# A decoder block on one core: the compression's row loads become steps of their own, and the gated unit's temporaries move to another buffer

## The chip, the cores and the metric

The kernel runs on one core of a Trainium2 chip. The metric is the device time of one execution in microseconds (us). Engines are named as in the profile: PE (matrix products; PEld is its weight load), DVE (vector), ACT (scalar functions; it also issues weight loads), POOL, and SP, which issues most of the other transfers.

## The reference

One decoder block over 512 tokens of width 1024: a half-step SwiGLU layer of inner width 2816, a mixing stage, a second SwiGLU layer, a gate with a per-layer embedding and a final norm. The mixing stage joins sparse attention (8 heads of 64, three branches) and a state-space mixer (S5) that ends in a gated unit. What the change touches, cut from the reference:

```python
def compress(kv, pe, w1, w2):            # done for keys and for values
    tok = arange(n_cmp)[:, None] * 16 + arange(32)[None, :]
    blk = kv[:, tok] + pe                # 31 windows of 32 tokens, stride 16
    ...
    return gelu(blk @ w1) @ w2
...
kc = compress(k_cmp, ...); vc = compress(v_cmp, ...)
...
def s5_mixer(...):
    ...
    y = gelu(y)
    return y * sigmoid(y @ w_glu + b_glu)
...
h = h + concat(o_nsa, o_s5) @ w_out
```

## The kernel before

All of it is one program on one core, tokens along the free axis, in tiles of 128 rows by 512 tokens. The two SwiGLU layers and the large projections split every weight tile into two parts, `hi` and `lo` (an ACT cast at L164 and a DVE subtraction at L166), and do three products for each pair of tiles. Weight tiles come through a ring of four buffers named `raw` (L107, issued by ACT).

The change lies in the mixing stage, at 400 to 620 us of the span. The stage is written as Python generators, each a chain of steps: `s` the state-space mixer, `q`, `Q` and `k` the projections with rotary embedding of queries and keys, `z` (`cmp_kv`) the projections of the keys and values that are to be compressed, `v` (`v_gates`) the values and branch gates, `p` and `t` the loading of queries and the scores of a block of 128 of them, `c` (`cmp_all`) the compression, `g` (`glu`) the gated unit, `f` the half of the output projection that reads the gated unit, `V` the products with the values. The string `PLAN` sets the order in which the steps are written down; a scheduler then places the instructions of each engine, earlier-written work first among what it holds to be ready. So a moved step shifts its neighbours on every engine too.

Steps pass results through small buffers with tags. Two tiles of one tag share memory, and the later one waits for all readers of the earlier. In the pool `tp` there is one buffer for each of `r1`, `r2`, `rb1`, `r3`; the rotary steps, the gated unit and the compression all use them.

- `cmp_kv` writes rotated keys to `kcd` (L1082) and values to `vcd` (L1087) in device memory.
- `windows` (L1114) reads them back in shifted copies: for each of two groups a tile `cst` in tag `r1` or `r2`, in two loads (L1118, L1119). Then DVE adds the position table `pe` (L1125) into `cs` (keys, tags `rb1` and `r3`) or into `turn` (values).
- `cmp_all` calls `windows` for keys and values in its first step; eight steps of matrix products `ps_A<-raw,cs` and `ps_A<-raw,turn` follow, and a last step with a gelu in `rb1`, a hidden tile `chid` in tag `acc` of the pool `npool` (L1153), and small products into `KAc` and `VLc`.
- `glu` runs a gelu over each of four tiles `yt` (function `gelu2`, L918: Square on ACT, a DVE step at L922, Tanh on ACT, a DVE step at L924), with its temporary `gt` in tags `r1`, `r2`, `r1`, `r2`. Then come sixteen products `ps_A<-yt,raw`, four for each of four results, the fourth of them reading the fourth `yt`. `f` needs all four results.

The first three gelus are written before the compression, the fourth well after it.

Of the kernel before, what the change touches and what calls it, by code (L numbers as in the profile page):

```python
# [10 lines left out]
F32 = mybir.dt.float32  # L11
# [8 lines left out]
SEQ = 512  # L20
# [56 lines left out]
def block_kernel(ctx: ExitStack, tc: tile.TileContext, a: dict, out: bass.AP):  # L77
# [14 lines left out]
    def bank(tag, shape=(128, 512), dt=F32):  # L92
        return psum.tile(list(shape), dt, tag=tag, name="ps_" + tag)
# [38 lines left out]
    def mm(o, lhsT, rhs, start, stop, **kw):  # L132
        return PE.matmul(o, lhsT, rhs, start=start, stop=stop, **kw)  # L133
# [10 lines left out]
    def unit(raw_only=False, keep=None, q=nc.scalar, after=None, at=None):  # L144
        i = unit_i[0] if at is None else at
        if at is None:
            unit_i[0] += 1
        w = UNIT_W[i]
        if i not in raws:
            load_unit(i, q)  # L150
        raw = raws.pop(i)
        if raw_only:
            return raw
        return split(raw, (slice(0, w),), keep, after)
# [25 lines left out]
    npool = ctx.enter_context(tc.tile_pool(name="npool", bufs=1, side="right"))  # L180
# [631 lines left out]
    with ExitStack() as f1:  # L812
# [5 lines left out]
        sp = s5c.enter_context(tc.tile_pool(name="s5c", bufs=1, side="right", reuse_waits="tile"))  # L818
# [25 lines left out]
    kcd = dram.tile([64, 2, SEQ], F32, tag="kcd", name="kcd")  # L844
    vcd = dram.tile([2, 64, SEQ], F32, tag="vcd", name="vcd")

    def mixer(ctx):
# [29 lines left out]
        tp = ctx.enter_context(tc.tile_pool(name="tmp", bufs=1, reuse_waits="tile"))  # L877
# [36 lines left out]
        def act(*args, **kw):  # L914
            with tc.issue_after(table[0].ins):
                S.activation(*args, **kw)

        def gelu2(o, x, w, tag):  # L918

            t = tp.tile([128, SEQ], F32, tag=tag, name="gt")[:, :w]  # L920
            act(t, x, AF.Square)
            V.scalar_tensor_tensor(t, t, 1 / 0.044715, x, OP.add, OP.mult)  # L922
            act(t, t, AF.Tanh, scale=math.sqrt(2 / math.pi) * 0.044715)
            V.scalar_tensor_tensor(o, t, 1.0, x, OP.add, OP.mult)  # L924
# [32 lines left out]
        cosr, sinr = turn[:, 0], turn[:, 1]  # L957
# [156 lines left out]
        def windows(src, i, dst):  # L1114
            ev = []
            for g in range(2):
                st = tp.tile([128, SEQ], F32, tag=f"r{g + 1}", name="cst")
                nc.sync.dma_start(st[0:64], src[g])  # L1118
                nc.sync.dma_start(st[64:128, 0:SEQ - 1], src[g, :, 1:SEQ])  # L1119
                ev.append(st.rearrange("p (j l r) -> p l j r", l=8, r=2)[:, :, :, 0])  # L1120
            sp = []
            for half, t in enumerate(dst):
                t = t.rearrange("p (l g j) -> p l g j", l=8, g=2)
                for g in range(2):
                    V.tensor_tensor(t[:, :, g], ev[g],  # L1125
                                    pe[:, i, 8 * half:8 * half + 8, None].to_broadcast([128, 8, 32]), OP.add)
                sp.append(t)
            return sp

        def cmp_all():  # L1130

            kt = [tp.tile([128, SEQ], F32, tag=n, name="cs") for n in ("rb1", "r3")]
            sps = windows(kcd.rearrange("(g r) a t -> g (r a) t", g=2), 0, kt), windows(vcd, 1, (cosr, sinr))
            yield
            ps = bank("A", (128, 256))
            for l in range(16):
                if l % 2 == 0:
                    raw = unit(True, at=next(at["cmp"]))
                lo, n = l // 8, 64 - l // 8
                for i in range(2):  # L1140
                    xs = sps[i][lo][:, l % 8].rearrange("p g j -> p (g j)")[:, lo:64]
                    w = (2 * i + l % 2) * 256
                    mm(ps[64 * i:64 * i + n], xs, raw[:, w:w + 256], l == 0, l == 15)
                if l % 2:
                    yield
            KBc = state["KBc"] = mp.tile([128, 4, 2, 128], FR, tag="turn", name="KBc")
            G.dma_start(KBc.rearrange("p q g j -> p (q g j)"), a["kbc"])
            ht = tp.tile([128, SEQ], F32, tag="r3", name="ht")[:, :256]
            gelu2(ht, ps, 256, "rb1")
            pt = bank("C", (128, 2, 128))  # L1150
            for m in range(2):
                PE.transpose(pt[:, m], ht[:, m * 128:m * 128 + 128], ident)
            hid = npool.tile([128, SEQ], F32, tag="acc", name="chid", bufs=1)[:, :256].rearrange("p (m c) -> p m c", m=2)  # L1153
            S.activation(hid, pt, AF.Copy, scale=0.5)
            hk, hv = hid[:, :, 0:63], hid[:, :, 64:127]
            p = bank("D", (64, 2, 32))
            for m in range(2):
                mm(p.rearrange("p g j -> p (g j)")[:, 0:63], w2[:, 0, m], hk[:, m], m == 0, m == 1)
            p = p[:, :, 0:31]
            kah = KAc[:, 0:128].rearrange("p (g i j) -> p g i j", g=2, i=2)  # L1160
            S.copy(kah[0:64, :, 0, 0:31], p)
            S.copy(kah[64:128, :, 0, 0:31], p)
            V.tensor_tensor(kah[0:64, :, 1, 0:31], p, kah[0:64, :, 0, 0:31].bitcast(F32), OP.subtract)
            for g in range(2):
                V.tensor_copy(KBc[0:64, :, g, 0:31],
                              kah[0:64, g:g + 1, 1, 0:31].bitcast(F32).to_broadcast([64, 4, 31]))
            for g in range(2):
                p = bank("D", (31, 64))
                for m in range(2):
                    mm(p, hv[:, m, 32 * g:32 * g + 31], w2[:, 1, m], m == 0, m == 1)  # L1170
                S.copy(VLc[0:31, g, 0:64], p)
                V.tensor_tensor(VLc[0:31, g, 64:128], p, VLc[0:31, g, 0:64].bitcast(F32), OP.subtract)


        def glu():
            for m in range(4):
                yt = yts[m]
                gelu2(yt, yt, SEQ, GT[m % 2])
                yield
            for m in range(4):  # L1180
                if m % 2 == 0:
                    raw = unit(True, at=next(at["glu"]))
                o = bank("A")
                for k in range(4):
                    q = (m * 4 + k) % 8
                    mm(o, raw[:, q * 128:(q + 1) * 128], yts[k], k == 0, k == 3)
                sg = mp.tile([128, SEQ], F32, tag="ra", name="sg", bufs=2)

                act(sg, o, AF.Tanh, scale=0.25, bias=bglu[:, m:m + 1])
                V.scalar_tensor_tensor(sg, sg, 1.0, yts[m], OP.add, OP.mult)  # L1190
                S.activation(oh[:, 4 + m], sg, AF.Copy, scale=0.25)
                V.scalar_tensor_tensor(ol[:, 4 + m], sg, 0.25, oh[:, 4 + m].bitcast(F32), OP.mult, OP.subtract)
                yield
# [132 lines left out]
        def values(qb, env):  # L1326
# [3 lines left out]
            for g in range(2):  # L1330
# [39 lines left out]
                for par in range(2):  # L1370
# [7 lines left out]
        envs = {qb: {} for qb in range(4)}  # L1378
        gens = dict(u=s5_input(), k=keys(), q=rotary("q0", qd[0], TQ[0]), Q=rotary("q1", qd[1], TQ[1]), z=cmp_kv(),
                    v=v_gates(), s=s5_all(), c=cmp_all(), g=glu(), f=out_half(range(4, 8)))  # L1380
        made = {"p": lambda b: queries(b, mp if b > 1 else ap_), "t": lambda b: scores(b, TS[b]),
                "x": lambda b: compressed(b), "V": lambda b: values(b, envs[b])}
        table.append(tc.keep_in_program_order(S.preload_act_table_set("exp_and_others")))
        for step in PLAN.split():
            if step == "close":
# [43 lines left out]
    for m in range(KT):  # L1429
# [3 lines left out]
        for k in range(2):  # L1433
            q = (m * 2 + k) % 8
# [16 lines left out]
    with tc.tile_pool(name="gate", bufs=2, reuse_waits="tile") as gp:  # L1451
# [8 lines left out]
        acc = npool.tile([128, SEQ], F32, tag="acc", name="accf", bufs=1)  # L1460
# [119 lines left out]
TU, TQ, TW, TY, TP = "AD", "AA", "C", "D", "D"  # L1580

TS = "AB", "AB", "BC", "BBBBBBBBBCBCBCBC"
GT = "r1", "r2"
STAGE = ("ra", "ra"), ("ra", "ra"), ("ra", "ra"), ("ra", "ra")

PLAN = """u u u k s s u k k q s q s Q p3 s s s k s Q s t3 t3 s t3 z t3 s s t3 s p3 s z t3 t3 s s t3 t3 s g t3 g t3 g t3
v t3 c v v c t3 v c c p2 t2 t3 t3 t2 p2 c c c t2 c c t2 t2 c v t2 t2 t2 t2 t2 t2 t2 t2 t2 g close p1 p1 p0 x3  # L1590
p0 g t2 g t2 g g t1 t1 x2 f S2 t1 f t1 t1 f t1 t1 f f t0 t0 R2 f x1 t0 R3 V3 V3 V3 V3 V3 V3 V3 V3 V3 V3 V3 V3
V3 V3 V3 V3 x0 f V3 t1 V3 V3 V2 V2 V2 V2 V2 t0 V2 V2 V2 V2 V2 S0 V2 R1 R0 V2 V2 V2 V2 V1 V1 V1 V1 V1 V1 V1
# [167 lines left out]
```

## Time and profile before

| | us |
|---|---|
| median of 3 runs (lowest, highest) | 1046.03 (1044.05, 1049.57) |
| the profiled execution, its own time | 1045.87 |
| its span | 1044.1 |
| DVE, ACT, POOL busy in the span | 823.1, 502.0, 160.5 |
| window loads `cst`, issue to landing, lowest/median/highest | 2.5/3.9/4.3 |

The profile's busy time of PE counts a matmul until its modelled end, and the records of neighbours overlap. So a waiting PE shows either as idle time ahead of a row, or as fewer matmuls in a stretch than in another with matmuls of the same size. A row of the timeline gives start, duration, engine, line and operation, and in brackets the idle time of that engine before it and what ended it.

### The profile page before, as it was taken

The page shows a single profiled execution, that of the slowest core. Times are in us where ns is not written, and L with a number is a line of the kernel's source. Part 1 is how long each engine was busy: PE and PEld are TensorE (multiplying, and loading weights), DVE is VectorE, ACT ScalarE, POOL GpSimd, SP SyncE. Part 2 cuts the span into 40 slices and gives each one's busy share as a digit, 9 for nine tenths or more (in the row PEclk, how much of TensorE's full clock was granted, in tenths as well). Part 3 has the DMA queues.
Part 4 walks back from the last instruction along what each step waited for, and adds up shares of the span by engine and source line. Part 5 has one row for each costly group of instructions (what it writes and reads, how often), then busy time and mean ns, then how long its engine had stood idle before and what let it go on. Part 6 is the DMA issues. An engine that isn't in the chain of part 4 may idle for free.

```text
span 1044.1 us, 15711 instructions
## 1 busy us (share of the span) xinstructions
PE 1030.6 (99%) x6049; PEld 876.9 (84%) x6049; DVE 823.1 (79%) x1381; ACT 502.0 (48%) x868; POOL 160.5 (15%) x181
## 2 busy tenths in 40 slices
PE   9999999999999999999999999999999999999997
PEld 7888888889889888776586688898899899899886
DVE  6798468988989766896689887996598588587666
ACT  6322232535336542477768855653365246245452
POOL 0003948207870200100000000000000000000001
PEclk9999999999999999999999999999999999999999
DMA  7424325636354648766610023434234333333412
GB/s 265 144 91 128 99 89 171 226 121 129 119 138 146 227 122 226 209 194 171 200 41 21 20 61 121 132 111 121 85 100 121 101 102 101 101 102 101 133 69 81
DMA packets 53114, 131.55 MB, mean 126 GB/s; under 512 B 10800, under 2 KB 19664, under 8 KB 53040
## 3 DMA queue, kind: packets, MB, share of 16 engines
q10 hardware_dynamic: 26352, 90.77, 27.4%
q0 software_dynamic: 6592, 18.48, 7.0%
q1 hardware_dynamic: 20096, 21.31, 6.7%
q8 instruction: 47, 0.77, 0.3%
q14 instruction: 27, 0.22, 0.1%
HBM read 114.39 MB, written 15.73 MB: 125 GB/s over the span
## 4 chain that ended last, share of the span: by engine, by line
PE 85%; DVE 5%; POOL 3%; DMA 3%; ACT 2%; issue 2%; SPq 0%; DVEq 0%; ACTq 0%; POOLq 0%
PE ps_A L133 25%; PE ps_C L133 24%; PE ps_B L133 20%; PE ps_D L133 15%; POOL ft L721 1%; POOL bt L720 1%; DMA qf<-qd 1%; DMA qd<-r 1%; DVE lo L166 1%; DMA kf<-kd 1%; DVE el L1359 0%; DMA cst<-kcd 0%; POOL ft L719 0%; DVE s L342 0%; POOL seen L559 0%
## 5 line engine op out<-in xcount | busy, mean ns | idle before, releaser
L164 ACT CAST hi<-raw 128x1024 fp32r<-128x1024 f32 (+2 forms) x143 | 144.4, 1010 | 253.3 <-PE ps_C L133 92.5
L133 PE MATMUL ps_C<-hq,hi 128*128 128x512 f32 x704 | 217.5, 390 | 0.2
L166 DVE TENSOR_TENSOR lo<-raw,hi 128x1024 fp32r<-128x1024 f32 (+2 forms) x143 | 173.4, 1213 | 42.5 <-ACT hi L164 41.5
L133 PEld LDWEIGHTS ps_C<-hq,hi 128*128 128x128 f32 x704 | 130.8, 188 | 28.1 <-DVE h L526 1.4
L133 PE MATMUL ps_C<-hq,lo 128*128 128x512 f32 x352 | 136.9, 389 | 0.0
L133 PE MATMUL ps_A<-xh,hi 128*128 128x512 f32 (+1 forms) x352 | 124.8, 355 | 0.4 <-ACT hi L164 0.4
L133 PE MATMUL ps_A<-xl,hi 128*128 128x512 f32 (+1 forms) x352 | 123.9, 352 | 0.0
L133 PE MATMUL ps_A<-xh,lo 128*128 128x512 f32 (+1 forms) x352 | 122.9, 352 | 0.2 <-DVE lo L166 0.2
L164 ACT CAST hi<-s 128x1024 fp32r<-128x1024 f32 x56 | 58.9, 1053 | 107.0 <-PE ps_D L133 60.9
L166 DVE TENSOR_TENSOR lo<-s,hi 128x1024 fp32r<-128x1024 f32 x56 | 70.6, 1261 | 20.3 <-ACT hi L164 20.2
L133 PEld LDWEIGHTS ps_C<-hq,lo 128*128 128x128 f32 x352 | 66.1, 188 | 13.8
L133 PEld LDWEIGHTS ps_A<-xh,hi 128*128 128x128 f32 x352 | 66.6, 189 | 10.3 <-ACT hi L164 0.7
L133 PEld LDWEIGHTS ps_A<-xh,lo 128*128 128x128 f32 x352 | 66.6, 189 | 9.2 <-DVE lo L166 0.4
L133 PEld LDWEIGHTS ps_A<-xl,hi 128*128 128x128 f32 x352 | 66.6, 189 | 9.3 <-DVE xl L192 0.3
L526 DVE SCALAR_TENSOR_TENSOR h<-ps_C,h 128x512 f32<-128x512 f32 x64 | 43.9, 686 | 36.5 <-PE ps_C L133 36.3
L133 PE MATMUL ps_B<-sh,lo 128*128 128x256 f32 x224 | 63.1, 282 | 0.3 <-DVE lo L166 0.3
L133 PE MATMUL ps_D<-sl,hi 128*128 128x256 f32 x224 | 63.1, 282 | 0.0
L133 PE MATMUL ps_B<-sh,hi 128*128 128x256 f32 x224 | 63.0, 281 | 0.0
L133 PE MATMUL ps_B<-sl,hi 128*128 128x256 f32 x224 | 62.9, 281 | 0.0
L133 PE MATMUL ps_B<-xh,hi 128*128 128x512 f32 (+1 forms) x168 | 62.9, 374 | 0.0
L133 PE MATMUL ps_D<-sh,hi 128*128 128x256 f32 x224 | 62.8, 280 | 0.0
L133 PE MATMUL ps_D<-sh,lo 128*128 128x256 f32 x224 | 62.6, 280 | 0.0
(434 smaller groups left out, 2472.1 us busy)
## 6 DMA issues: line engine op xcount, KB each, us to landing
raw<-in_wpack ACTq DMA_DIRECT2D x168, 512.0 KB, 3.6
si<-s5i POOLq DMA_DIRECT2D x8, 512.0 KB, 5.3
so<-s5o POOLq DMA_DIRECT2D x8, 512.0 KB, 5.7
h<-in_xT SPq DMA_DIRECT2D x8, 256.0 KB, 4.5
s5i<-fs POOLq DMA_DIRECT2D x1, 2048.0 KB, 11.4
xraw<-in_xT SPq DMA_DIRECT2D x8, 256.0 KB, 3.6
s5o<-gt POOLq DMA_DIRECT2D x1, 2048.0 KB, 13.3
s5i<-tcs POOLq DMA_DIRECT2D x2, 1024.0 KB, 10.2
```

The costliest lines, as they stand in the source:

```text
L133: return PE.matmul(o, lhsT, rhs, start=start, stop=stop, **kw)
L164: p, q = S.copy(hi[:, c], raw[:, c]), None
L166: q = V.tensor_tensor(lo[:, c], raw[:, c], hi[:, c].bitcast(F32), OP.subtract)
L526: V.scalar_tensor_tensor(h[:, m, :], o[m], 0.5, h[:, m, :], OP.mult, OP.add)
L720: G.tensor_tensor(bt, b2[:, 1], bc(psn[:, e]), OP.mult)
L721: G.tensor_tensor(ft[:, :, s_, :], ft[:, :, s_, :], bt, OP.add)
```

## The change

`windows` becomes a generator with two steps: the loads, then the adds. `cmp_all` gets two steps more: loads of the keys' rows; their adds and the loads of the values' rows; the values' adds. `PLAN` gets two more `c`. The first stands right behind the second `z`, the second behind the first gelu of the gated unit; the old first place now holds the values' adds. The temporaries of the gated unit move from `r1` and `r2` to the one buffer `acc` of `npool`, which `chid` also uses. No instruction is added or removed.

```diff
-            t = tp.tile([128, SEQ], F32, tag=tag, name="gt")[:, :w]
+            t = (npool if tag == "acc" else tp).tile([128, SEQ], F32, tag=tag, name="gt", bufs=1)[:, :w]
...
                 ev.append(st.rearrange("p (j l r) -> p l j r", l=8, r=2)[:, :, :, 0])
+            yield
             sp = []
...
-            return sp
+            yield sp
...
-            sps = windows(kcd.rearrange("(g r) a t -> g (r a) t", g=2), 0, kt), windows(vcd, 1, (cosr, sinr))
+            kw, vw = windows(kcd.rearrange("(g r) a t -> g (r a) t", g=2), 0, kt), windows(vcd, 1, (cosr, sinr))
+            next(kw)
+            yield
+            sps = [next(kw)]
+            next(vw)
+            yield
+            sps.append(next(vw))
             yield
...
-GT = "r1", "r2"
+GT = "acc", "acc"
...
-PLAN = """u u u k s s u k k q s q s Q p3 s s s k s Q s t3 t3 s t3 z t3 s s t3 s p3 s z t3 t3 s s t3 t3 s g t3 g t3 g t3
+PLAN = """u u u k s s u k k q s q s Q p3 s s s k s Q s t3 t3 s t3 z t3 s s t3 s p3 s z c t3 t3 s s t3 t3 s g t3 c g t3 g t3
```

The added lines move all later lines down: L1125 becomes L1126, L1261 becomes L1268.

Three places show what that does to the engines' orders. The first is ACT at about 439 us of the span, where the first gelu (`gt`) and the copies of the state-space mixer (`ysb`, `so`) meet the first softmax exponentials of the last query block (`ps_B,den`). Before:

```order
L1066 CAST KA<-kf 128x512
L164 CAST hi<-raw 128x840
L107 DMA raw<-in_wpack 128x1024
L1010 COPY ysb<-ps_D 64x2x8x16 x2
L998 COPY so<-so 64x4x128 x2
L916 ACTIVATE ps_B,den<-ps_B,nmax 128x512 x2
L916 ACTIVATE gt<-yt 128x512
```

And with the change:

```order
L1066 CAST KA<-kf 128x512
L916 ACTIVATE gt<-gt 128x512
L164 CAST hi<-raw 128x840
L1010 COPY ysb<-ps_D 64x2x8x16 x2
L998 COPY so<-so 64x4x128 x2
L107 DMA raw<-in_wpack 128x1024
L916 ACTIVATE ps_B,den<-ps_B,nmax 128x512 x2
```

The first gelu no longer stands behind the exponentials, and the issue of a weight load has moved behind the copies.

The second is DVE where the keys' windows get their table (`cs<-cst,pe`). Before, the second pair stands among the copies of `v_gates` (`VL`, `gp`):

```order
L924 SCALAR_TENSOR_TENSOR yt<-gt,yt 128x512
L1106 SCALAR_TENSOR_TENSOR VL<-ps_A,ri,VL 128x4x64
L1108 TENSOR_SCALAR gp_3607<-ps_A,ri 128x24
L1261 TENSOR_REDUCE nmax<-ps_B 128x1
L1125 TENSOR_TENSOR cs<-cst,pe 128x8x32 x2
L1261 TENSOR_REDUCE nmax<-ps_C 128x1
```

With the change both pairs stand around the last weight split of `v_gates`, before any `VL`:

```order
L1126 TENSOR_TENSOR cs<-cst,pe 128x8x32 x2
L985 TENSOR_TENSOR t_4452<-t_4452,t_4453 128x256
L1086 TENSOR_TENSOR ra<-ps_A,rb 128x512
L988 SCALAR_TENSOR_TENSOR vv<-r_121,t_4452 128x64 x4
L1268 TENSOR_REDUCE nmax<-ps_B 128x1
L166 TENSOR_TENSOR lo<-raw,hi 128x560
L1268 TENSOR_REDUCE nmax<-ps_B 128x1
L1126 TENSOR_TENSOR cs<-cst,pe 128x8x32 x2
```

The values' adds follow six rows further on, behind the third gelu's first DVE step. On SP the second pair of the keys' loads moves from behind four later pairs of query loads to right behind the first pair.

The third is PE behind the compression, in the gated unit's products (`ps_A<-yt,raw`), with scores of the third query block (`ps_B<-KA,QA`) between them. Before they come in four blocks of four:

```order
L133 MATMUL ps_A<-yt,raw 128x512 x4
L133 MATMUL ps_B<-KA,QA 128x384
L133 MATMUL ps_B<-KB,QB 128x384
L133 LDWEIGHTS identb
L133 MATMUL ps_B<-maskq,identb 128x128
L133 MATMUL ps_A<-yt,raw 128x512 x4
L133 MATMUL ps_D<-chid,w_3621 64x63 x2
```

With the change the first two blocks have three products each; the fourth `yt` comes only behind `chid`, since its gelu now shares the buffer, and 45 rows further on stands the rest:

```order
L133 MATMUL ps_C<-QA,KAc 128x512
L133 MATMUL ps_A<-yt,raw 128x512 x2
L133 MATMUL ps_C<-QA,KA 128x512
L133 MATMUL ps_B<-KA,QA 128x256
L133 MATMUL ps_B<-KB,QB 128x256
L133 MATMUL ps_B<-KA,QA 128x256
L133 MATMUL ps_B<-KB,QB 128x256
L133 LDWEIGHTS identb
L133 MATMUL ps_B<-maskq,identb 128x2x128
L133 MATMUL ps_A<-yt,raw 128x512 x8
```

So ten of sixteen products move behind the compressed keys and behind the first scores of the second query block. Three of the first six `f` blocks (twelve products `ps_A<-oh,hi` and the like each) move with them into the products with the values.

## The prediction

> **What bounds the kernel now.** I read the page first, then the busy time by stretches, then the chain of work that ended last, and then the timelines of the stretches that stood out.
>
> ```profile
> span 1044.1 us, 15711 instructions
> PE 1030.6 (99%) x6049; PEld 876.9 (84%) x6049; DVE 823.1 (79%) x1381; ACT 502.0 (48%) x868; POOL 160.5 (15%) x181
> PE 85%; DVE 5%; POOL 3%; DMA 3%; ACT 2%; issue 2%; SPq 0%; DVEq 0%; ACTq 0%; POOLq 0%
> ```
>
> PE is busy for all but 13.5 us (1044.1 - 1030.6) and carries 85% of the chain. The change takes no matmul away, so it can only win back time in which PE waits, or add such time. The stretches show where that is.
>
> ```profile
> core 0: us, PE busy (x) PEld busy (x) DVE busy (x) ACT busy (x) POOL busy (x), PEclk, DMA share, GB/s
> 440.00:450.00 10.00, 8.48 (x48) 6.25 (x48) 9.27 (x20) 5.42 (x13) 0.92 (x2) 0.86 0.64 212
> 460.00:470.00 10.00, 10.00 (x82) 7.54 (x81) 9.81 (x24) 6.86 (x14) 0.00 (x0) 1.00 0.79 222
> 480.00:490.00 10.00, 8.78 (x61) 5.58 (x60) 9.44 (x19) 6.29 (x15) 0.00 (x0) 1.00 0.36 99
> 490.00:500.00 10.00, 10.00 (x70) 6.74 (x70) 4.09 (x10) 4.81 (x16) 0.57 (x1) 1.00 0.94 329
> 560.00:580.00 20.00, 19.76 (x77) 12.56 (x76) 16.94 (x39) 16.93 (x34) 0.00 (x0) 1.00 0.00 1
> 580.00:600.00 20.00, 19.85 (x81) 12.38 (x81) 18.27 (x32) 17.99 (x37) 0.00 (x0) 1.00 0.08 27
> 620.00:640.00 20.00, 20.00 (x91) 16.27 (x90) 13.04 (x25) 10.38 (x17) 1.03 (x1) 1.00 0.49 161
> ```
>
> Three places matter. At 440 to 450 us PE idles 1.52 us and its granted clock falls. At 480 to 490 us, where the compression begins, it idles 1.22 us. From 560 to 600 us idle time is small, but PE starts only 77 and 81 matmuls in 20 us, where it starts 91 at 620 to 640 us, nearly all of the same width: it waits in pieces too short to show as idle, since ACT and DVE are at 17 to 18 of 20 us.
>
> **The windows' loads, the part that the change is about.** The chain before the compression, and the two PE rows and one DVE row that answer to it:
>
> ```profile
> 474.44 0.69 DVE yt L924
> 476.09 4.12 DMA cst<-kcd
> 481.93 2.61 DMA cst<-vcd
> 480.31 1.11 DVE L1125 TENSOR_TENSOR cs<-cst,pe 128x256 f32<-128x256 f32 x2 [3.31 <-DMA cst<-kcd]
> 482.65 0.62 PE L133 MATMUL ps_A<-raw,cs 128*64 128x256 f32 x2 [0.69 <-PE ps_A L133]
> 485.27 0.43 PE L133 MATMUL ps_A<-raw,turn 128*64 128x256 f32 x1 [0.53 <-DVE turn L1125]
> ```
>
> The third gelu holds the buffer `r1` until 475.13 us. Only then does the second keys' load start, DVE stands 3.31 us for it, the values' load follows the adds, and PE waits 0.69 and 0.53 us: 1.22 us, all the idle time of that stretch. With the change the buffers are free of gelus, and the adds stand ahead of most of `v_gates`, whose last 24 products PE ran as cover while these loads came. The wait goes: **-1.2 us**, bounds -1.2 and 0. The DVE stall of 3.31 us goes too, but was covered except for this. What is late next is the weights: 490 to 500 us has 0.94 of the DMA engines busy at 329 GB/s, so the compression cannot run ahead of its eight weight tiles by much.
>
> On SP the move puts one more pair of loads ahead of a pair of query loads. Of that:
>
> ```profile
> 459.83 0.46 SPq L1118
> 460.34 0.59 SPq L1119
> 464.81 0.63 ACT L1239 ACTIVATE QB<-qf 64x512 fp32r<-64x512 f32 x1 [3.02 <-DMA qf<-qd]
> ```
>
> The pair costs 0.46 + 0.59 = 1.05 us of issue, and ACT, which already waits 3.02 us there, waits up to that much longer; scores' exponentials queue behind it. PE was busy all through that stretch (460 to 470 us: 10.00 of 10), on projections, so I take 0, bounds 0 and +1.1.
>
> **The first gelu.** At 440 us the order of ACT decides:
>
> ```profile
> 441.38 1.02 DVE L166 TENSOR_TENSOR lo<-raw,hi 128x840 fp32r<-128x840 f32 x1
> 442.43 0.33 ACTq L107 DMA_DIRECT2D raw<-in_wpack  x1
> 443.09 0.75 ACT L1010 COPY ysb<-ps_D 64x256 f32<-64x256 f32 x2 [2.86 <-DVE nmax L1261]
> 443.86 1.25 ACT L998 COPY so<-so 64x512 f32<-64x512 f32 x2
> 445.13 0.66 ACT L916 ACTIVATE ps_B<-ps_B,nmax 128x512 f32<-128x512 f32 x1
> 445.96 0.50 PE L133 MATMUL ps_B<-KA,QA 128*128 128x512 f32 x1 [1.37 <-ACT ps_B L916]
> 439.46 0.68 DVE L1067 TENSOR_TENSOR KB<-kf,KA 64x512 fp32r<-64x512 f32 x1 [0.71 <-ACT KA L1066]
> 448.59 0.69 DVE L922 SCALAR_TENSOR_TENSOR gt<-gt,yt 128x512 f32<-128x512 f32 x1 [0.54 <-ACT gt L916]
> 447.00:448.00 1.00, 1.00 (x5) 0.62 0.53 203
> 448.00:449.00 1.00, 1.00 (x7) 0.50 0.01 2
> 450.00:451.00 1.00, 1.00 (x14) 0.67 0.52 153
> ```
>
> PE waits 1.37 us for a score bank that the exponentials at 445.13 us free. These stand behind two pairs of copies, these behind the issue of a weight load at 442.43 us, and that waited for the `lo` subtraction, over at 442.40 us; so ACT stood 2.86 us. Now that issue stands behind the copies, which run during the subtraction. In return the first gelu is put ahead: its first DVE step (0.69 us) fits into the 0.71 us that DVE idles at 439 us, while its second step and a step of the state-space mixer, some 0.65 us each (0.68 and 0.69 us in these rows, less a little overlap), push `lo` from 442.40 to about 443.7 us. The issue then takes 0.66 us (442.43 to 443.09), and the exponentials start at about 444.35 instead of 445.13 us: 0.8 us earlier. Two matmuls that PE did ahead of the wait now stand behind it, 2 x 20/91 = 0.45 us. Net **-0.4 us**. The bounds are wider: all of the idle time gone (-1.5) with the clock's dip that follows it (-1.7), together -3.2; or, with a second dip, +1.7. The dip: after this wait the clock is at one half for 3.4 us (0.38/0.5 us of the slice at 447, all of 448 to 450, 0.33/0.5 of that at 450), which costs half of that, 1.7 us. I leave it in both.
>
> [...]
>
> **The gated unit's buffer.** `gt` in `acc` costs nothing for the first three gelus; they come one after another anyway. The fourth must wait for `chid`'s last reader, and with it ten of sixteen products `ps_A<-yt,raw`. They were what PE did while ACT and DVE worked off scores. Prices:
>
> ```profile
> 498.20 0.42 PE L133 MATMUL ps_B<-KA,QA 128*128 128x384 f32 x1
> 498.68 0.42 PE L133 MATMUL ps_B<-KA,QA 128*128 128x384 f32 x1
> 499.19 3.65 PE L133 MATMUL ps_A<-yt,raw 128*128 128x512 f32 x8
> 502.28 0.74 PE L133 MATMUL ps_B<-KA,QA 128*128 128x384 f32 x1
> 517.98 0.63 PE L133 MATMUL ps_B<-KAc,QA 128*128 128x64 f32 x4
> 518.45 0.42 PE L133 MATMUL ps_C<-KA,QA 128*128 128x384 f32 x1
> L916 ACT ACTIVATE ps_B<-ps_B,nmax 128x384 f32<-128x384 f32 x5 | 2.8, 550 | 1.5 <-DVE nmax L1261 1.5
> L916 ACT ACTIVATION_READ_ACCUMULATOR ps_B<-ps_B,nmax 128x1 f32 x5 | 1.0, 195 | 0.0
> L164 ACT CAST hi<-raw 128x1024 fp32r<-128x1024 f32 x3 | 3.1, 1040 | 2.7 <-DMA raw<-in_wpack 2.7
> ```
>
> From the compression's last product to the first held-back product, PE has with the change eleven scores of 384 keys (0.48 us each, 498.20 to 498.68), six products of the gated unit (3.09 us for four from 499.19 to 502.28, so 0.77 each, recorded twice each), sixteen products with `KAc` (0.47 us for four), and some 1 us of small ones: 5.3 + 4.6 + 1.9 + 1 = 12.8 us. ACT has in the same stretch eleven exponentials (550 + 195 ns), three weight casts (1040 ns), and four gelu steps and a few small copies, by the 0.66 us of a 512-wide step at 445.13 us some 3.2 us: 8.2 + 3.1 + 3.2 = 14.5 us. So PE runs short of work by 14.5 - 12.8: **+1.7 us**. Behind `chid` on ACT stand the exponentials, and PE waits for the banks that they free. `chid` itself now stands behind two weight casts in a row, with one exponential pair between them before, and the second waits for a load that can be issued only when the compression is over. Bounds: 0, if the casts' weights are there, and 1.7 + 2.7 = +4.4, if the 2.7 us that the casts waited come on top.
>
> Nothing is lost of that work: it comes later. Three blocks of twelve products, 36 x 20/91 = 7.9 us of PE, move with it from a stretch in which PE was full into the products with the values, where ACT is short. There 560 to 580 us has 91 - 77 = 14 matmuls too few, 14 x 20/91 = 3.1 us that could be filled. The blocks come in lumps of 2.6 us while the waits are spread, so I take half, **-1.5 us**, bounds -3.1 and 0.
>
> **Sum.** -1.2 + 0 - 0.4 + 1.7 - 1.5 = -1.4 us. Against the profiled execution's 1045.87 us that is 1044.5 us; the median of the runs lies 0.2 us above that execution, so 1044.6 us. The lower ends add up to -7.5, the upper to +7.2.
>
> **Rivals.**
>
> 1. The blocks fill the waits: the stretch behind the compression costs nothing, the products with the values take the full 3.1 us, and at 440 us wait and dip go. -1.2 - 3.1 - 3.2 = -7.5: 1038.5 us. For it speaks that 580 to 600 us has ten matmuls too few as well; against it, that the dip needs only a short wait and that ACT stays at 17 of 20 us there.
> 2. ACT holds up PE behind the compression: `chid` and all exponentials stand behind a cast that waits for its weights, at the place where DMA is fullest (0.94). The wait of 4.4 us comes whole, and the clock dips, 1.7. If the values' stretch gives nothing back, -1.2 - 0.4 + 4.4 + 1.7 = +4.5: 1050.5 us. It turns slower once the starved stretch costs more than 1.6 us with nothing given back, or more than 3.1 us with the 1.5. For it speaks the 2.7 us of waiting in the casts' row; against it, that PE has four scores and six products of the gated unit, 6.5 us of work, between the compression's end and `chid`. [...]
> 3. The change does not do what it says: the loads are early, but the compression's products start no earlier, since weights and `v_gates` stand ahead of them. Then only the order shuffles: between 0 and +1, 1046.5 us. Against it: at 482.65 us the weights of these products were there, and PE waited for `turn` alone.
>
> **How the numbers follow.** Forecast 0.55, first rival 0.18, second 0.15, third 0.12. A difference of 0.5%, 5.2 us, is about what a measurement of this kernel can tell from no change. Faster by more than that (below 1040.8) is the larger part of the first rival: 0.17. Slower by more (above 1051.3) is the worse half of the second: 0.08. The rest is 0.75. The range leaves out the far halves of the first two rivals: 1039.5 to 1049.5 us.
>
> **What would show it.** Right: no DVE idle on `cst`, and no PE idle ahead of the compression's first products; the first exponentials of the last query block some 0.8 us ahead of where they stood against the copies; `ps_A<-oh,hi` among `ps_D<-eh,VL`, and in the stretch of the first products with values more than 77 matmuls in 20 us. Wrong: PE idle on ACT between `ps_D<-chid` and the held-back `ps_A<-yt,raw`, a second dip of the clock, or waits for `raw` in the compression.

## The result, and the profile after

| | before | changed |
|---|---|---|
| median of 5 runs (lowest, highest), us | 1046.03 (1044.05, 1049.57) | 1053.81 (1053.11, 1056.94) |
| its profiled execution: own time, span, us | 1045.87, 1044.1 | 1056.94, 1055.2 |
| mean granted clock of that execution | 0.997 | 0.992 |

The changed kernel is slower: ratio 1.0081, 95% interval 1.0064 to 1.0099. That is above the whole range given, and on the other side of the kernel before.

First the head of the page after, with the shares of the chain of work that ended last:

```profile
span 1055.2 us, 15683 instructions
PE 1034.7 (98%) x6048; PEld 879.7 (83%) x6049; DVE 823.8 (78%) x1381; ACT 501.9 (48%) x868; POOL 160.2 (15%) x181
...
PE 84%; DVE 4%; DMA 4%; POOL 3%; issue 2%; ACT 2%; SPq 0%; DVEq 0%; ACTq 0%; POOLq 0%
```

PE shows 1034.7 us busy against 1030.6 before, with the same matmuls. So some of them took longer: the loss is not idle time alone. The busy time by stretches, after, says where (columns as before: stretch, its length, busy time and instructions of PE, PEld, DVE, ACT and POOL, then PEclk, the DMA share and GB/s):

```profile
440.00:450.00 10.00, 8.86 (x64) 6.76 (x62) 9.64 (x20) 6.00 (x13) 1.31 (x2) 1.00 0.57 189
450.00:460.00 10.00, 7.80 (x58) 6.00 (x58) 9.74 (x16) 6.54 (x14) 1.08 (x2) 1.00 0.58 165
460.00:470.00 10.00, 9.14 (x71) 6.68 (x70) 7.31 (x20) 4.80 (x12) 0.43 (x1) 1.00 0.56 173
480.00:490.00 10.00, 10.00 (x75) 7.18 (x73) 6.04 (x14) 6.80 (x16) 0.00 (x0) 1.00 0.51 130
510.00:520.00 10.00, 8.02 (x35) 5.64 (x34) 6.69 (x16) 7.27 (x22) 0.00 (x0) 0.66 0.37 116
520.00:530.00 10.00, 10.00 (x31) 6.38 (x32) 5.74 (x13) 5.91 (x18) 0.00 (x0) 0.66 0.18 54
```

Three things differ from before. The stretch at 480 us, where the compression begins, has no idle PE any more (it had 1.22 us). At 440 to 470 us PE idles 1.14, 2.20 and 0.86 us. And behind the compression, at 510 to 530 us, PE idles 2 us and then runs at a granted clock of 0.66, with 35 and 31 matmuls in 10 us.

The first of these is what the change is about. DVE's first add of a loaded row and PE's first products of the compression, after:

```profile
465.48 1.09 DVE L1126 TENSOR_TENSOR cs<-cst,pe 128x256 f32<-128x256 f32 x2 [2.56 <-DMA cst<-kcd]
484.81 0.43 PE L133 MATMUL ps_A<-raw,cs 128*64 128x256 f32 x1
484.82 0.43 PE L133 MATMUL ps_A<-raw,turn 128*64 128x256 f32 x1
```

PE no longer waits there: those rows have no bracket. DVE still stands for a load, 2.56 instead of 3.31 us, but earlier, on the first pair of adds.

The second, at 440 to 460 us, is a chain through four engines (DVE, then SP, ACT and PE, after; the bracket is the engine's idle time before the row and what ended it):

```profile
437.22 0.69 DVE L922 SCALAR_TENSOR_TENSOR gt<-gt,yt 128x512 f32<-128x512 f32 x1
441.37 0.68 DVE L924 SCALAR_TENSOR_TENSOR yt<-gt,yt 128x512 f32<-128x512 f32 x1
446.02 0.69 DVE L1054 TENSOR_TENSOR r<-r,r 128x512 f32<-128x512 f32 x1
446.74 0.33 SPq L1056 DMA_DIRECT2D qd<-r  x1
451.52 0.61 SPq L1243 DMA_DIRECT2D qf<-qd  x1
455.47 0.63 ACT L1246 ACTIVATE QB<-qf 64x512 fp32r<-64x512 f32 x1 [2.66 <-DMA qf<-qd]
457.38 0.62 ACT L998 COPY so<-so 64x512 f32<-64x512 f32 x1
458.05 0.44 PE L133 MATMUL ps_D<-so,z 128*64 128x128 f32 x4 [1.46 <-ACT so L998]
```

Both steps of the first gelu now stand ahead of rotary's last add. That add's store `qd` goes out at 446.74 us, where it went at 444.82 us before; the query load `qf` follows at 451.52 instead of 448.58 us (0.7 us of each is there already at 410 us, where the profiles still run alike). ACT now stands 2.66 us for it, the `so` copies stand behind, and PE waits 1.46 us for those.

The third, behind the compression (ACT and PE, after):

```profile
507.53 1.04 ACT L164 CAST hi<-raw 128x1024 fp32r<-128x1024 f32 x1 [2.85 <-DMA raw<-in_wpack]
508.48 0.38 ACT L1161 ACTIVATE chid<-ps_C 128x256 f32<-128x256 f32 x1
515.21 0.63 ACT L916 ACTIVATE gt<-yt 128x512 f32<-128x512 f32 x1
508.91 0.45 PE L133 MATMUL ps_D<-chid,w 128*64 128x63 f32 x4 [0.76 <-ACT chid L1161]
511.06 0.45 PE L133 MATMUL ps_C<-KA,QA 128*128 128x384 f32 x1 [0.26 <-ACT ps_C L916]
513.37 0.69 PE L133 MATMUL ps_C<-KA,QA 128*128 128x384 f32 x1 [1.61 <-ACT ps_C L916]
523.26 3.62 PE L133 MATMUL ps_A<-yt,raw 128*128 128x512 f32 x4
```

ACT stands 2.85 us on a weight cast whose tile has not landed; `chid` and all exponentials are behind it. PE waits 0.76 us for `chid`, then 0.26 and 1.61 us for score banks. The fourth gelu starts at 515.21 us, and only at 523.26 us come held-back products of the gated unit. Then the clock, in finer slices of the same stretch:

```profile
512.00:513.00 1.00, 0.00 (x0) 0.00 (x0) 0.77 (x1) 0.96 (x5) 0.00 (x0) 1.00 0.70 283
513.00:514.00 1.00, 0.63 (x2) 0.50 (x2) 1.00 (x4) 0.87 (x4) 0.00 (x0) 0.59 0.03 12
514.00:526.00 12.00, 11.90 (x45) 8.59 (x43) 6.49 (x18) 6.89 (x20) 0.00 (x0) 0.50 0.14 45
526.00:527.00 1.00, 1.00 (x4) 0.44 (x3) 0.62 (x1) 0.09 (x1) 0.00 (x0) 0.58 0.00 0
```

The clock is at one half for 0.41/0.5 + 12 + 0.42/0.5 = 13.66 us. That costs half of it, 6.8 us (an estimate), since PE is busy for nearly all of that time (11.90 of 12 us) and its products follow each other nearly twice as slowly: from a 384-wide `KA` product to its `KB` product it is 0.47 us at 516.80 us, and 0.26 us at 504.19 us, at the full clock.

### The profile page after: what moved, and what is told of

It reads as the page before. It is cut to its first block, busy times and chain, and to the rows that moved or that the text cites. A ratio compares the mean times of both kernels' runs of the same rounds, so it can differ in the third digit from the quotient of the medians.

```text
span 1055.2 us, 15683 instructions
## 1 busy us (share of the span) xinstructions
PE 1034.7 (98%) x6048; PEld 879.7 (83%) x6049; DVE 823.8 (78%) x1381; ACT 501.9 (48%) x868; POOL 160.2 (15%) x181
## 4 chain that ended last, share of the span: by engine, by line
PE 84%; DVE 4%; DMA 4%; POOL 3%; issue 2%; ACT 2%; SPq 0%; DVEq 0%; ACTq 0%; POOLq 0%
PE ps_A L133 24%; PE ps_C L133 24%; PE ps_B L133 20%; PE ps_D L133 15%; POOL ft L721 1%; DMA qf<-qd 1%; POOL bt L720 1%; DMA kf<-kd 1%; DMA qd<-r 1%; DMA raw<-in_wpack 1%; DVE lo L166 1%; DMA kd<-r 1%; DMA h<-in_xT 0%; DVE nmax L1268 0%; POOL ft L719 0%
## 5 line engine op out<-in xcount | busy, mean ns | idle before, releaser
L133 PEld LDWEIGHTS ps_A<-xh,hi 128*128 128x128 f32 x352 | 66.4, 189 | 10.4 <-ACT hi L164 0.7
```

## The experiments

**Theory and rivals.** Theory 1: the loss sits behind the compression and comes from the buffer; the fourth gelu's temporary shares `acc` with `chid`, so PE runs short of work there and its clock halves (0.50 above). Rival A: it comes from the first gelu, ahead of rotary's adds. Rival L: it comes from the load steps.

For each run the table gives its comparison with the kernel before, and two times (us) from the timeline of its profiled execution, both from the first product `ps_D<-so,z` at about 410 us: to the start of the compression's last product, and to the start of the last product that reads `KBc`, a score product that stands a few rows ahead of the end of the products with the values. The kernel before has 87.8 and 190.8.

| run | median us | ratio to before (95%) | mean clock of its runs | to the end of the compression | to the end of the values |
|---|---|---|---|---|---|
| changed | 1053.81 | 1.0081 (1.0064 to 1.0099) | 0.9930 | 88.9 | 201.1 |
| changed, again | 1052.19 | 1.0066 (1.0052 to 1.0081) | 0.9930 | 87.8 | 197.6 |
| buffer alone | 1053.60 | 1.0068 (1.0045 to 1.0091) | 0.9948 | 88.7 | 194.5 |
| load steps alone | 1047.72 | 1.0024 (1.0012 to 1.0036) | 0.9976 | 91.2 | 195.1 |
| fourth gelu in `r2` | 1045.26 | 0.9997 (0.9986 to 1.0009) | 0.9984 | 87.3 | 190.8 |
| `chid` in `r2` | 1046.01 | 0.9997 (0.9985 to 1.0008) | 0.9979 | 87.9 | 191.4 |
| fourth gelu alone in `acc` | 1049.24 | 1.0033 (1.0019 to 1.0048) | 0.9965 | 88.6 | 193.5 |
| casts behind `chid` | 1049.45 | 1.0030 (1.0018 to 1.0042) | 0.9969 | 88.5 | 193.3 |
| rotary first | 1044.35 | 0.9991 (0.9982 to 0.9999) | 0.9975 | 86.9 | 191.1 |
| rotary first, again | 1044.71 | 0.9990 (0.9980 to 0.9999) | 0.9974 | 86.5 | 190.0 |
| loads at once | 1045.48 | 1.0003 (0.9991 to 1.0014) | 0.9975 | 85.4 | 188.0 |

The kernel before had a mean clock of 0.9975 to 0.9977 in the three groups of runs.

**Buffer alone.** The kernel before, with only this (`GT` holds the tags of the gelus' temporaries):

```diff
-GT = "r1", "r2"
+GT = "acc", "acc"
```

and the line in `gelu2` that lets a tag name `acc`.

> The kernel before with one edit: all four gelus keep their temporary in `acc`; the compression's loads stay in the step that uses them, and the plan is the old one. Theory 1 (the buffer does everything; the load steps move nothing, because the loads were held by `r1` and `r2` and not by their place in the plan): the time of the changed kernel, 1053 to 1055 us, ratio to before 1.007 to 1.009. Rival L (the load steps, with their extra SP work ahead of the qd and qf transfers, make the loss): within 0.2% of before, 1046.

Measured: 1053.60 us, as the changed kernel. Written out by the scheduler, this kernel has the same instructions in the same order on all five engines as the changed one: once the temporaries have left `r1` and `r2`, the loads move to the same places with the old plan. Its profiled execution happened to be one without the dip, at 1049.62 us; the other three took 1052.28 to 1055.45. Its stretch behind the compression, first a PE row, then the slice that was at 0.50 above:

```profile
511.68 0.44 PE L133 MATMUL ps_C<-KA,QA 128*128 128x384 f32 x1 [1.36 <-ACT ps_C L916]
514.00:526.00 12.00, 11.57 (x48) 6.80 (x47) 10.16 (x25) 9.69 (x28) 0.00 (x0) 1.00 0.20 64
```

The same starvation, at full clock: 194.5 us to the end of the values, 3.7 more than before. The changed kernel's 201.1 us is 6.6 more than that, and its dip costs 6.8 us by the clock. Rival L falls: the loss comes without the load steps.

**Load steps alone.** The changed kernel with the old `GT`:

```diff
-GT = "acc", "acc"
+GT = "r1", "r2"
```

> The changed kernel with the gelus' temporaries back in `r1` and `r2`: the compression's loads are steps of their own at the new places of the plan, and nothing else. The first gelu then waits for `r1` and so stays behind rotary's last adds; the fourth stays ahead of `chid`. Theory 1 (the steps by themselves take away the waits for the loaded rows, 1.2 us of TensorE, and the whole loss belongs to the buffer): 1043 to 1045.5, ratio 0.997 to 1.000, with no dip at 500 to 530 us. Rival L (loads that run earlier collide with the qd and qf transfers and the weights): 1047 to 1050. Rival N (the loads are held by `r1` and `r2` until the gelus are done with them, so nothing moves): within 0.1% of before, with the products of the compression still waiting at 485 us.

Measured: 1.0024. Theory 1 and rival N miss it; the time fits rival L's, and the trace shows a second reason beside rival L's. ACT, DVE and PE rows:

```profile
464.69 0.63 ACT L916 ACTIVATE gt<-yt 128x512 f32<-128x512 f32 x1 [5.27 <-DVE cs L1126]
476.53 1.10 DVE L1126 TENSOR_TENSOR turn<-cst,pe 128x256 f32<-128x256 f32 x2 [3.13 <-DMA cst<-vcd]
480.74 0.37 PE L133 MATMUL ps_A<-hi,xh 128*128 128x280 f32 x1 [2.11 <-DVE gp L1108]
```

With the loads early in `r1` and `r2`, a gelu waits for the adds that read these buffers, and ACT stands 5.27 us in front of it. The values' adds stand on DVE 3.13 us before their load is there; `gp` is behind them, and PE waits 2.11 us for that, behind which the clock dips: 0.83 from 480 to 490 us, which would be 0.17 x 10/0.5 = 3.4 us at one half (an estimate). The last of these loads took 5.1 us from its issue to its landing, where the slowest before took 4.3, and the DMA share is 1.10 at 470 to 480 us (0.77 before), so a part of the loss may be the collision that rival L names. At these places in the plan the steps cost time unless the gelus leave the two buffers; that early loads don't need it is shown by the last run below. The reading comes from the trace; no run took one of these waits away alone.

**Fourth gelu in `r2`.** The changed kernel with:

```diff
-                gelu2(yt, yt, SEQ, GT[m % 2])
+                gelu2(yt, yt, SEQ, GT[m])
...
-GT = "acc", "acc"
+GT = "acc", "acc", "acc", "r2"
```

> The changed kernel, but the fourth gelu's temporary is in `r2` again, so that it doesn't wait for the bank pass of `chid`; the first three stay in `acc`. Theory 1 (the loss sits behind the compression: the fourth gelu behind `chid`, ScalarE behind a weight cast that waits for its DMA, TensorE starved and then four windows at half clock): 1045 to 1049, at least 6 us under the changed kernel; no half clock between 500 and 530 us, products with the values at about 500 to 516 in blocks of 4. Rival A (the first gelu ahead of rotary's last adds, and the late qf loads and KB copies that follow, make the loss): 1051 to 1054, with no idle of TensorE on `chid`.

Measured: 0.9997, the kernel before. The windows from 500 to 530 us:

```profile
500.00:510.00 10.00, 10.00 (x35) 5.06 (x35) 5.66 (x10) 6.15 (x14) 0.01 (x1) 1.00 0.71 230
510.00:520.00 10.00, 10.00 (x46) 5.48 (x45) 7.75 (x17) 8.08 (x22) 0.00 (x0) 1.00 0.53 162
520.00:530.00 10.00, 10.00 (x61) 8.22 (x61) 8.23 (x19) 7.32 (x25) 0.00 (x0) 1.00 0.12 46
```

No idle PE and a full clock, although ACT's cast still waits 1.32 us for its weights there. This edit alone gives back the whole loss. The "four windows" of the expectation are the 13.66 us at one half above, 4.0 times the 3.42 us of the dip in the kernel before. The expectation named the gated unit's products as those "with the values"; they come in four blocks of four again. Idle time at 440 to 480 us stays at 4.9 us, and the compression still ends 0.5 us earlier than before (87.3 against 87.8). So what the first gelu costs there is about what the loads gain in this profile, and rival A falls as the cause of the loss.

**`chid` in `r2`.** The changed kernel, all four gelus in `acc`, with:

```diff
-            hid = npool.tile([128, SEQ], F32, tag="acc", name="chid", bufs=1)[:, :256]...
+            hid = tp.tile([128, SEQ], F32, tag="r2", name="chid")[:, :256]...
```

> The changed kernel with all four gelus in `acc`, and `chid` in `r2` instead of `acc`, so that the fourth gelu is no longer tied to it. If the tie is what costs, and not `acc` as a place: as the run with the fourth gelu in `r2`, 1044 to 1047, with no half clock at 500 to 530 us. If `acc` or the early order of the first gelus costs by itself: 1049 or more.

Measured: 0.9997, no idle PE and clock 1.00 from 500 to 530 us, although ACT's cast waits 2.77 us for its weights there, nearly as long as in the changed kernel (2.85). It is the tie between the two tiles that costs, not `acc` as a place, and without the tie a cast that waits cost nothing here.

**Fourth gelu alone in `acc`.** The kernel before, with `GT` of four entries:

```diff
-GT = "r1", "r2"
+GT = "r1", "r2", "r1", "acc"
```

> The kernel before, but the fourth gelu alone has its temporary in `acc`; the first three keep `r1`, `r2`, `r1`, so the compression's loads stay late. Theory 1 (loss behind the compression): 1052 to 1056, with TensorE at half clock for 7 to 14 us between 505 and 530 us. Rival A (the loss comes from the first gelu): 1046 to 1048. A third way: the two halves need each other, since only the early start of the compression brings `chid` to the cast that waits; then also 1046 to 1048, and the fourth gelu alone costs under 2 us.

Measured: 1.0033, a loss of 3.6 us by the medians and about half of the changed kernel's. None of the three expectations holds: it lies between theory 1 and the other two. ACT's cast and `chid`, and PE:

```profile
505.79 1.04 ACT L164 CAST hi<-raw 128x1024 fp32r<-128x1024 f32 x1 [2.18 <-DMA raw<-in_wpack]
506.74 0.38 ACT L1154 ACTIVATE chid<-ps_C 128x256 f32<-128x256 f32 x1
512.41 0.44 PE L133 MATMUL ps_B<-KA,QA 128*128 128x384 f32 x1 [0.48 <-ACT ps_B L916]
```

The tie is there, the starvation is there (2.7 us more than before by the end of the values), but in shorter pieces: 1.27 us of idle time from 500 to 530 us where the changed kernel has 3.05, no wait for `chid`, and a full clock there in this profile. Of the eleven executions the four slowest, 1050.25 to 1051.60 us, are the four with a mean clock of 0.994 or 0.995, so some may have a dip. By these profiles the early part adds to the length of the waits, and the long dip comes with it. Two causes that are worth 0 and 3.6 us alone are worth some 7 together.

**Casts behind `chid`.** The changed kernel, with ACT's casts of the output projection's weights ordered behind `chid`:

```diff
-            S.activation(hid, pt, AF.Copy, scale=0.5)
+            state["chid"] = S.activation(hid, pt, AF.Copy, scale=0.5).ins
...
-                        with tc.issue_after(state["oh"]) if done and m == 4 else nullcontext():
+                        with tc.issue_after(state["chid"] if not done else state["oh"]) if not done or m == 4 else nullcontext():
```

> The changed kernel with one edit: the casts of the next weights on ScalarE are ordered behind the activation that makes `chid`, so that a cast that waits for its DMA can no longer stand in front of `chid`. The fourth gelu still waits for the pass of `chid`. Theory 1 with the queue behind the cast as the cause: `chid` 2 to 3 us earlier, no dip of the clock or one short one, 1045 to 1049. Rival (the tie between `chid` and the fourth gelu is enough by itself, since the blocks of products still come as 8 at the end): 1050 to 1054, with the dip still there.

Measured: 1.0030, 0.5 us above theory 1's range and as much below the rival's. ACT and PE:

```profile
505.90 0.37 ACT L1161 ACTIVATE chid<-ps_C 128x256 f32<-128x256 f32 x1
513.86 0.44 PE L133 MATMUL ps_C<-KA,QA 128*128 128x384 f32 x1 [0.80 <-ACT ps_C L916]
457.67 0.44 PE L133 MATMUL ps_D<-so,z 128*64 128x128 f32 x4 [1.90 <-ACT so L998]
```

`chid` comes 2.6 us earlier, the idle time behind the compression is in pieces of at most 1.08 us, there is no dip in this profile from 400 to 620 us (clock 1.00 throughout), and the mean clock of the runs is 0.9969, near that of before. So the cast that waits for its weights makes the long wait behind the compression, and without it the dip there is gone. That the length of a wait alone makes a dip is not shown: the last row, at 457 us, is a wait of 1.90 us, longer than any behind the compression of the changed kernel, and no dip follows it. The shortage of work itself stays: 2.5 us by the end of the values.

**The changed kernel again,** unedited.

> The changed kernel once more, unedited, for the spread of its executions. Theory 1 with the dip as a part of the loss that only comes when the weights land late: most executions at a mean clock of 0.992 to 0.995 and 1052 to 1057 us, some at 0.997 or above and 1048 to 1051; so two groups with some 4 us between them, and a loss of about 4 us that is there without the dip. Rival (the loss is idle time and late products alone, the clock only an accompaniment): one group round 1054, with no relation between its clock and its time.

Measured: six runs at 0.991 to 0.994 and 1051.45 to 1054.41 us: one group, none without the dip. With the runs above, 14 of 15 executions of this order have a mean clock of at most 0.994, and the other one 0.999 and the lowest time of all. So the expected two groups are there only as 14 to 1. The dip in this profile, by its first slice, its body and its last:

```profile
512.00:513.00 1.00, 1.00 (x8) 0.70 (x8) 0.76 (x2) 1.00 (x4) 0.00 (x0) 0.73 0.73 299
514.00:520.00 6.00, 5.90 (x22) 4.52 (x21) 3.98 (x9) 3.44 (x12) 0.00 (x0) 0.50 0.01 3
522.00:523.00 1.00, 1.00 (x6) 0.86 (x4) 0.00 (x0) 0.71 (x2) 0.00 (x0) 0.65 0.00 0
```

It lasts 0.27/0.5 + 9 + 0.35/0.5 = 10.24 us and costs 5.1. The rival's other half, no relation between clock and time, is not settled by six runs of one group.

**Rotary first.** The fourth gelu in `r2`, and the first gelu's first DVE step ordered behind rotary's last add:

```diff
-            V.scalar_tensor_tensor(t, t, 1 / 0.044715, x, OP.add, OP.mult)
+            with tc.issue_after(behind) if behind else nullcontext():
+                V.scalar_tensor_tensor(t, t, 1 / 0.044715, x, OP.add, OP.mult)
...
-            V.tensor_tensor(a2, a2, b2, OP.add)
+            state["turned"] = V.tensor_tensor(a2, a2, b2, OP.add).ins
...
-                gelu2(yt, yt, SEQ, GT[m % 2])
+                gelu2(yt, yt, SEQ, GT[m], None if m else state["turned"])
...
-GT = "acc", "acc"
+GT = "acc", "acc", "acc", "r2"
```

> As the run with the fourth gelu in `r2`, and the first DVE step of the first gelu is ordered behind rotary's last add, so that the two sums that go to qd leave VectorE as early as before. Theory 1 for 440 to 480 us (the idle of TensorE there, 4.9 us in that run, comes from the late sums: late qd and qf transfers, a KB copy on ScalarE that waits 2.7 us for them with the copies of `so` behind it): under 2.5 us of idle in that stretch and 1042 to 1044. Rival (the exponentials behind `nmax` and the products with `so` are late for another reason, the order on VectorE of the adds of the loaded rows): idle stays at 4 to 5 us, 1045 to 1046.

> The version with the fourth gelu in `r2` and the first gelu behind rotary's last add, once more, to see whether it beats the kernel before: 0.998 to 0.9995 of it if the first time was no accident, and 0.990 to 0.993 of the changed kernel.

Measured: 0.9991, and again 0.9990 of the kernel before, 1.0 us, far less than 0.5%; both intervals end at 0.9999. PE's waits at 440 to 480 us in the first profile are two:

```profile
445.41 0.50 PE L133 MATMUL ps_B<-KA,QA 128*128 128x512 f32 x1 [1.37 <-ACT ps_B L916]
467.56 0.50 PE L133 MATMUL ps_B<-KA,QA 128*128 128x512 f32 x1 [0.76 <-ACT ps_B L916]
```

2.1 us in place of 4.9: PE's wait for the `so` copies (1.54 us in the run with the fourth gelu in `r2`) is gone, as theory 1 for that stretch has it, while the medians are 0.4 and 0.7 us above its range. The wait of 1.37 us at 445 us is that of before, back with its dip (clock 0.83 from 440 to 450 us). The second profile has 2.77 us of idle PE there, above theory 1's 2.5: ACT stands 4.51 us for a later pair of query loads, and PE waits 1.85 us for exponentials behind that. So the expectation for that stretch holds in one profile of two. By its medians this is the best of the versions tried.

**Loads at once.** `GT` as before, and the three new steps together behind the last `z`:

```diff
-... s p3 s z c t3 t3 s s t3 t3 s g t3 c g t3 g t3
- v t3 c v v c t3 ...
+... s p3 s z c c c t3 t3 s s t3 t3 s g t3 g t3 g t3
+ v t3 v v c t3 ...
```

> Temporaries in `r1` and `r2` as before, and all three new steps stand right behind the last `z` ahead of the gelus, so that the loads come first and the gelus wait for `r1` and `r2` until the loaded rows have been used. Theory 1 (what costs is a gelu that ends late, whatever makes it late): the products with the values come in blocks of 4, 8 and 4, some starvation of TensorE behind the compression, 1045 to 1049. Rival (early loads are worth more than the order of the gelus): 1042 to 1044.

Measured: 1.0003, so the rival's gain didn't come. Theory 1 has the time and the blocks of 4, 8 and 4, but not the starvation: PE has no idle time from 500 to 530 us. The loads come early here with the temporaries in `r1` and `r2`, and the compression ends earlier than in any other profile (85.4 us). Its profiled execution is its fastest, 1043.24 us of 1043.24 to 1047.40: from 440 to 500 us PE waits only three times there, 0.98, 0.17 and 0.40 us. What the slower ones lose is open.

## Why the prediction was wrong

- **Loads of the windows, -1.2 us: right.** PE's two waits ahead of the compression are gone. But the text counted on both halves of the change; the runs show that the buffer alone moves the loads to these places, and that the steps alone cost 2.2 us at the median.
- **One more pair of loads ahead of a query load, 0 to +1.1 us: right for ACT, open for PE.** ACT waits 4.05 us there in place of 3.02. PE's waits at 460 to 480 us, none longer than 0.7 us, add up to 1.55 where there were none before, but the first gelu's delay is in them. With rotary first, where that delay is gone, the same stretch still has a wait of 0.76 and of 1.85 us in the two profiles. So 0 was too low, and what this pair alone costs PE no run shows.
- **First gelu, -0.4 us: wrong by about 2 us.** Its own steps hold: the exponentials come 0.9 us earlier (0.8 named), and PE's wait for their bank is 1.14 us in place of 1.37. But the working followed the first gelu to `lo` and to ACT's copies only, and left out what else stood behind it on DVE: rotary's last adds, and behind them `qd`, `qf`, the copy into `QB` and the `so` copies. In two of the three profiles with this order that made 4.9 and 4.6 us of idle PE at 440 to 480 us in place of 1.52 with a dip of 1.7; in the third the early idle was 2.7 us with a dip (clock 0.96 from 440 to 480 us). By the end of the compression that is 0 to 1.1 us later than before, with the loads' gain of 1.2 us in it. So this term, with what the pair of loads above costs in it, was +1.2 to +2.3 us; its upper bound of 1.7 stood for another reason.
- **The gated unit's buffer, +1.7 us less 1.5 given back: the step that failed**, together with the clock that it left out. The mechanism was named: the fourth gelu behind `chid`, PE without its filling work, ACT behind a cast that waits. From the end of the compression to the end of the values the kernel before takes 103.0 us. The buffer-alone profile, which has no dip, takes 105.8; the changed kernel's two take 112.2 and 109.8, less the dips' 6.8 and 5.1, so 105.4 and 104.7. That is +1.7 to +2.8 us, where the two terms made +0.2. What failed is the part given back. The first and the last `KBc` product, before and then after:

```profile
547.87 0.58 PE L133 MATMUL ps_C<-QB,KBc 128*128 128x512 f32 x1
600.90 0.39 PE L133 MATMUL ps_C<-QB,KBc 128*128 128x512 f32 x1
549.09 0.58 PE L133 MATMUL ps_C<-QB,KBc 128*128 128x512 f32 x1
611.93 0.39 PE L133 MATMUL ps_C<-QB,KBc 128*128 128x512 f32 x1
```

Between them the changed kernel has 51 more matmul rows with `ps_A` (63 against 12). 36 are the three blocks of `f`: 36 x 20/91 = 7.9 us of work, 8.4 by the starts of the rows. The other 15 are three blocks of scores that came along; twelve of them are 256 wide and start 0.12 us apart, about 2.0 us in all (an estimate from these starts). That is 9.9 to 10.4 us of work, and the stretch takes 62.84 - 53.03 = 9.8 us longer. So 0.1 to 0.6 us came back instead of 1.5: the moved work hardly filled any waits. Why not is open; no run tested it. Behind the compression the shortage then cost some 2 to 3 us, above the 1.7 and within its bounds.
- **The clock: the missing term.** The forecast had no dip at that place. The second rival had one, of 3.4 us, at a cost of 1.7. The gated unit's term should have had one: it came as 13.66 and 10.24 us, 6.8 and 5.1 us of cost, in two of three profiles. Over all runs, by (1 - mean clock) x span, the clock takes 7.4 us in the changed kernel in both sets, and 2.4 to 2.6 us before: about 5 us of the 6.6 to 7.8 us of loss. This is an estimate from the clock; no run took the dip away and left the waits. In the changed kernel's profile the three parts add up: 1.1 us to the end of the compression, 2.4 from there and 6.8 by the clock are the 10.3 us by which it is late at the end of the values.
- **The second rival was what happened:** `chid` behind the waiting cast, PE idle on ACT behind `ps_D<-chid`, a dip of the clock, and nothing to speak of given back. Its 4.4 us for the wait was too much (3.05 us of idle PE from 500 to 530 us) and its dip a quarter to a third of the real one; 1050.5 us was 3.3 us too low. Against it the text held the 6.5 us of work that PE has before `chid`. PE did that work and was through with it 0.76 us before `chid`; but the idle time that followed came from the exponentials, which queue behind the same cast, and none of PE's work covered those.
- **The third rival** came in part: counted from the first `ps_D<-so,z`, the compression's first product starts at 74.0 us in the changed kernel and 72.9 in its second profile, against 72.6 before. So the loads were early and the products not. But what held them was not the weights or `v_gates`, as that rival had it; by the trace it was the time lost at 440 to 470 us, to the late query loads.

Of the signs named beforehand, all those for "wrong" came but one (there are no waits for `raw` inside the compression), and of those for "right" PE's waits ahead of the compression, which are gone, and the matmuls among the products with values (89 in 20 us from 560 us, against 77). But that last sign misled: ten of the 89 belong to the moved blocks of scores, eight of them 256 wide. The first exponentials of the last query block start 34.2 us after that first `ps_D<-so,z`, against 35.1 before: 0.9 us earlier, as named. Not right: DVE's wait for `cst` moved instead of going.

## What to carry to other kernels

When a temporary moves to another buffer, list the readers of everything that has ever used that buffer, and place the new owner's last possible start by them: here one tile that shared its place with `chid` held back ten of sixteen products that PE lived on. And when an early start is bought, follow each engine's queue behind the work that now stands first, to the transfers and back, not only to the next row. A starved stretch of PE should be priced with its clock: with waits of up to 1.6 us and a dip behind them, this shortage cost 7 to 8 us (the changed kernel); with pieces of at most 1.1 us and no dip in the profile it cost 3 to 4 (casts behind `chid`). And moved work should not be counted as filling waits until its own width, and what it brings along, have been counted.

## What the runs showed of the hardware

The dips of the clock were of different length. After 1.37 us of idle time (the kernel before) one lasted 0.38/0.5 + 2 + 0.33/0.5 = 3.42 us; with 2.63 us in three pieces within 5.2 us (the changed kernel) one lasted 13.66 us, and with 2.35 us likewise (again) 10.24 us: 4.0 and 3.0 times 3.42 us. PE was shown busy for 11.90 of 12 us within the long one, so it stayed at half clock while its engine had work, narrow products among it (`ps_B<-KAc,QA`, 64 wide). And a dip is not certain: 1.37 us in one piece at 446 us brought none with the load steps alone (clock 1.00 from 440 to 460 us), 1.36 us in one piece none in the buffer-alone profile (1.00 from 510 to 530 us), nor did 1.90 us at 457 us with the casts behind `chid` (1.00 from 450 to 470 us), so the length of a wait does not settle it. No run added a wait or filled one by itself, so that the waits make the dip rests on these pairs of profiles.

No wait ahead of the three dips was longer than 1.61 us. Why they took 3.42, 10.24 and 13.66 us, no run here shows.
